# Pre-norm weight rows made by transposes and kept in PSUM, transposes of x ahead of the plain products, and other planned times for the first loads

## The chip, the cores and the metric

The kernel runs on one core of a Trainium2 chip. The metric is the device time of one execution in microseconds (us); of several runs the median counts. A core has five engines that run side by side, each with its own queue, in order: TensorE (PE, with its weight loads as PEld), VectorE (DVE), ScalarE (ACT), GpSimd (POOL) and SyncE (SP), which here issues most of the DMAs. They meet only through semaphores. Matrix products and transposes are PE's; in this kernel they write to banks of 128 x 512 float32 in PSUM, which ACT and DVE empty. The other tiles are in SBUF.

## The reference

One layer with four token mixers side by side, merged by gates. Only its head matters for the change: the residual stream (16 meta tokens, then 1024 tokens of width 1024) is normalised with the weight `pre_norm_g`, and one wide product makes the inputs of all branches.

```python
h_res = jnp.concatenate([meta, x], axis=1)          # L = 16 + 1024 rows of D_MODEL = 1024
...
def rms_norm(x, g):
    xf = x.astype(jnp.float32)
    y = xf * lax.rsqrt(jnp.mean(xf * xf, axis=-1, keepdims=True) + EPS)
    return (y * g.astype(jnp.float32)).astype(x.dtype)
...
h = rms_norm(h_res, pre_norm_g[i])
z = h @ w_in[i]
(pv, pg, cq, ckv, kr, mg, cu, cg, sbcx, sg, gl) = split_cols(z)
...
m = (gts[:, :, 0] * y_a + gts[:, :, 1] * y_b + gts[:, :, 2] * y_c + gts[:, :, 3] * y_d)
h_res = h_res + rms_norm(m @ w_o[i], post_norm_g[i])
```

## The kernel before

**A planner sets the order.** The code does not issue instructions as it runs. `record` (L287) notes each with its engine, tiles and dependences, and `flush` (L326) plays all noted instructions through a table of costs (`cost`, L266) and issues them in the order that results; `issue` (L321, called in L324) is why nearly every row of the profile has line 324. Each engine takes the ready instruction with the lowest number, where `ahead` lifts some. A load counts as landed at a planned time (L406): the pipe's time, the bytes and 4500 ns; `slow` adds `extra` nanoseconds to the moment at which its users may be planned. The table only orders instructions. On the chip the engines wait for semaphores, whatever the table thought.

**Dummies.** Where PE has nothing ready, the planner appends a transpose of the identity into an unused bank, `ps_w` (L381 to 386, `keep_busy`), and counts it as 108 ns. This goes on until the last product of the first pair of blocks has run (L1183). Once appended, a dummy stands in PE's queue and is executed, whether PE has something better to do by then or not.

**The start** (L698 to 770). SP loads eight tiles of x (128 tokens each, 512 KB), the weight row `gB`, `pre_norm_g` broadcast to 128 partitions (512 KB written), and the first columns of `w_in` (`raw_kv`, two blocks of 320 KB). For tiles t and t + 4 together, `parts(t)` makes squares with sums on ACT (`junk`), the reciprocal root on DVE and POOL (`rsx`), the scaling by `rsx` and `gB` on DVE, in halves of 512 columns (`scaled`, L714), and then the transposes: `operand_of` (L721) makes four 128 x 128 transposes on PE into a bank (two `ps_x` and one `ps_y` in turn), copies the result on ACT to the high part of an operand and subtracts on DVE for the low part. Every float32 operand here is such a pair, and a product is three matmuls for each 128 rows. `sums_of(t)` forms four differences of the x tiles on POOL, in place, and transposes them into the operands T1, T2 and T4; the wide product is done in the manner of Strassen with seven products for eight (`unit`, L568), whose weight blocks `prep` (L540) makes by sums on DVE (`ss`) and splits on ACT and POOL. `meta` does the same for the 16 meta tokens, `xm`.

**The plain products** (`plain`, L613) compute the columns `ckv` and `kr` directly, 96 matmuls for U0 (the first 256 tokens of each half) and 96 for U1. The order of the calls before: `parts(0)`, `parts(1)`, plain U0, `parts(2)`, `parts(3)`, `meta`, plain U1, then `sums_of` for all t, then the last transposes into T3, then the units. In a unit, the bank `ps_pc` is used twice: the eviction `z` on DVE must have read the first result before the second product may be added to it, and it needs `u3`, an eviction of `ps_pb`.

Everything after (the remaining blocks, attention over 8 heads, the output products) is not touched in the code.

Of the kernel before, what the change touches and what calls it, by code (L numbers as in the profile page):

```python
# [21 lines left out]
F32 = mybir.dt.float32  # L22
# [3 lines left out]
ALU = mybir.AluOpType  # L26
# [4 lines left out]
P = 128  # L31
D = 1024
# [161 lines left out]
class Plan:  # L194
# [131 lines left out]
    def flush(self):  # L326
# [38 lines left out]
        while events:  # L365
# [11 lines left out]
            for e in self.free:  # L377
# [3 lines left out]
                if o is None:  # L381
                    if e == "PE" and self.idle and self.ops[self.idle[1]]["end"] is None:
                        order.append(self.idle[0])
                        self.free[e] = t + 108
                        heapq.heappush(events, (self.free[e], 1, 0))
                    continue
                ready[e].remove((o["prio"], o["i"]))
# [13 lines left out]
                if o["op"] == "dma_start":  # L401
                    if self.pipe is None:
                        self.pipe = max((x["done"] for x in self.ops if x["op"] == "dma_start"
                                         and "done" in x and x["start"] <= t), default=0)
                    o["done"] = self.pipe = max(self.pipe, t) + o["bytes"]
                    land = self.pipe + o["bytes"] + 4500  # L406
                    o["end"] = land + o["extra"]
                    if o["eng"] != "POOL":
                        self.landed.append(land)
                    heapq.heappush(events, (land, 1, 0))  # L410
# [19 lines left out]
def trunk_kernel(ctx, tc, a):  # L430
# [76 lines left out]
    def bank(tag="x"):  # L507

        return psum.tile([P, 512], F32, tag=tag, bufs=2 if tag == "x" else 1, name=f"ps_{tag}")
# [103 lines left out]
    def plain(w, c0, n, out):  # L613

        for j, bs in enumerate(((B11, B21), (B12, B22))):
            for i, m in enumerate((P, 64)):
                ps = bank(("pa", "pb", "pc", "pd")[2 * j + i])[:m, :n]
                for h, b in enumerate(bs):
                    product(ps, w[h][i], b, c0, n, h == 0, h == 1)
                with plan.ahead(EVAC):  # L620
                    out(i, j, ps, None, None)
# [62 lines left out]
    def wload(i, c, n=2 * P):  # L684

        t = raw("raw")
        SP.dma_start(t[:, :, :n], w_in[:, KH * i:KH * (i + 1), c:c + n])
        return t
# [3 lines left out]
    def load_x(t):  # L692
# [2 lines left out]
                 raw("x").rearrange("p k c -> p (k c)") if t == 0 else  # L695
                 wp.tile([P, D], F32, tag="blk", bufs=7, name="x"))
        SP.dma_start(xt[t], a["x"][0, P * t:P * (t + 1), :])
    load_x(0)  # L698
    load_x(4)
    gB = tp.tile([P, D], F32, tag="conv", bufs=1, name="gB")  # L700
    SP.dma_start(gB, a["pre_norm_g"][0].partition_broadcast(P))
    load_x(1)
    load_x(5)
    raw_kv = [wload(i, C_CKV, P + 32) for i in range(2)]
    for t in (2, 6, 3, 7):
        load_x(t)
    ssx = const.tile([P, 16], F32, name="ssx")
    rsx = const.tile([P, 16], F32, name="rsx")

# [3 lines left out]

    def scaled(x_, t):  # L714
        n = x_.shape[0]
        for s in (slice(0, 512), slice(512, D)):
            DVE.scalar_tensor_tensor(x_[:, s], x_[:, s], rsx[:n, t:t + 1], gB[:n, s], op0=ALU.mult, op1=ALU.mult)

    turn = [0]

# [30 lines left out]
            operand_of(b, t, src)  # L751

    def meta():
        xm = wp.tile([NM, D], F32, tag="blk", bufs=7, name="xm")
        SP.dma_start(xm, a["meta_tokens"])
        square(xm, 8)
        rsqrt_mean(rsx[:NM, 8:9], ssx[:NM, 8:9], D)
        scaled(xm, 8)
# [39 lines left out]
        w_kv[i].append(kr[:, i])  # L798
    parts(1)
    out_kv = [out_raw(("ckv", "kr"), *u) for u in (U0, U1)]  # L800
    plain(w_kv, *U0, out_kv[0])
    parts(2)
    parts(3)
    meta()
    plain(w_kv, *U1, out_kv[1])
    for t in range(4):
        sums_of(t)
    for t in range(4):
        operand_of(T3, t, xt[t + 4][:, :512])
    prow = w1([P, P], name="prow")  # L810
    for r0, n, src in rows:
# [358 lines left out]
        (C_MG, ("mg0", "mg1"), out_silu),  # L1170
        (C_MG + 2 * P, ("mg2", "mg3"), out_silu),
    ] + [(C_GL + P * g, g, None) for g in range(0, 32, 2)]
    w = prep(pairs[0][0])
    for i, (_, names, kind) in enumerate(pairs):
        with plan.ahead(3000):
            nxt = prep(pairs[i + 1][0]) if i + 1 < len(pairs) else None
# [394 lines left out]
```

## Time and profile before

| | |
|---|---|
| median of 3 runs | 1052.6 us (1050.21 to 1053.01) |
| the profiled execution | 1056.61 us |
| its span, first to last instruction | 1054.6 us |
| mean granted clock of PE | 0.990 |
| first transpose of x on PE | 16.42 us |
| first product of the first unit | 62.27 us |
| last dummy | 72.6 us |

A row of a time line gives the start, the length, the engine, the line, the operation with its tiles as out<-in, the shapes, how many follow each other, and in brackets how long the engine was idle before it and what it waited for. Lengths of matmuls are those of the pipeline; the distance from one start to the next is what one costs PE. A row of groups ends with the busy time in us, the mean of one in ns, and the idle time ahead of it; a row of one tile's operations has the count, then the shortest, median and longest in ns, then the first and last start. A row of a window has the window, its length, then the busy time of PE, PEld, DVE, ACT and POOL with counts, the granted clock (1.00 is full), the DMA share and GB/s.

### The profile page before, as it was taken

The numbers are of one execution on the slowest core, as the hardware profiler recorded it, in microseconds if no ns is written. First come the engines' busy times: TensorE is split into PE (matmuls) and PEld (weight loads), VectorE is DVE, ScalarE is ACT, GpSimd is POOL, SyncE is SP. The second block draws the span as 40 slices with busy tenths as digits, with TensorE's granted clock in tenths as the row PEclk, the third lists the DMA queues.
The fourth block names the chain that finished last, engine by engine and source line by source line (L and its number), as shares of the span: only waits on it lengthen the run. The fifth ranks groups of instructions, "written<-read, shape, count | busy, mean of one in ns | idle before, by whom it ended". The sixth has DMA issues, their size and how long they took to land.

```text
span 1054.6 us, 15499 instructions
## 1 busy us (share of the span) xinstructions
PE 1024.6 (97%) x5310; PEld 858.8 (81%) x5310; DVE 725.0 (69%) x1078; ACT 428.1 (41%) x861; POOL 640.1 (61%) x582
## 2 busy tenths in 40 slices
PE   9999999999999999999999999989998989999997
PEld 9999899889888787887777778868887877678885
DVE  4865499699998998899644554266776787586232
ACT  5452333334433444533544444216655544233111
POOL 4847766657767777798867966226687866412000
PEclk9999999999999999999999999999999989999999
DMA  7033545856576655756487564987568654596221
GB/s 249 20 88 114 156 159 189 255 189 217 156 253 215 223 172 168 240 189 197 149 252 217 194 195 135 321 279 241 152 172 251 181 151 141 143 357 232 97 80 60
DMA packets 124703, 196.33 MB, mean 186 GB/s; under 512 B 19466, under 2 KB 78969, under 8 KB 123280
## 3 DMA queue, kind: packets, MB, share of 16 engines
q1 hardware_dynamic: 120016, 178.56, 53.9%
q10 hardware_dynamic: 4320, 15.73, 3.9%
q8 instruction: 42, 0.69, 0.3%
q0 software_dynamic: 288, 1.05, 0.2%
q14 instruction: 37, 0.30, 0.1%
HBM read 125.78 MB, written 69.53 MB: 185 GB/s over the span
## 4 chain that ended last, share of the span: by engine, by line
PE 44%; DVE 7%; DMA 4%; issue 3%; POOL 2%; ACT 0%; SPq 0%; POOLq 0%; ACTq 0%; DVEq 0%
PE ps_o L324 12%; PE ps_y L324 9%; PE ps_s L324 7%; PE ps_pb L324 4%; PE ps_pc L324 4%; PE ps_pa L324 4%; DVE conv L324 3%; PE ps_pd L324 2%; DMA whl<-w_out_mla 1%; PE ps_x L324 1%; DMA kt<-kr 1%; DMA th<-th 1%; DVE ss L324 1%; POOL S L324 1%; POOL A L324 0%
## 5 line engine op out<-in xcount | busy, mean ns | idle before, releaser
L324 PE MATMUL ps_pb<-T,S 128*128 128x512 f32 (+2 forms) x792 | 178.4, 367 | 1.7 <-DVE u L324 1.4
L324 PE MATMUL ps_pa<-B,A 128*128 128x512 f32 (+2 forms) x792 | 174.3, 364 | 0.0
L324 POOL TENSOR_TENSOR S<-ss,S 128x512 fp32r<-128x512 f32 x84 | 122.8, 1476 | 81.9 <-ACT S L324 77.5
L324 PEld LDWEIGHTS ps_pb<-T,S 128*128 128x128 f32 x792 | 135.6, 190 | 28.1 <-DVE u L324 2.0
L324 POOL TENSOR_TENSOR A<-raw,A 128x512 fp32r<-128x512 f32 x84 | 123.8, 1482 | 54.7 <-ACT A L324 51.9
L324 PEld LDWEIGHTS ps_pa<-B,A 128*128 128x128 f32 x792 | 135.4, 189 | 24.5 <-issue 0.5
L324 DVE SCALAR_TENSOR_TENSOR conv<-conv,par 128x512 f32<-128x512 f32 x120 | 149.2, 1243 | 2.1
L324 POOL TENSOR_TENSOR pt<-p,pt 128x512 fp32r<-128x512 f32 (+4 forms) x112 | 103.0, 948 | 25.9 <-ACT pt L324 16.2
L324 PE MATMUL ps_y<-bo,whl 128*128 128x512 f32 x288 | 86.6, 408 | 2.5 <-DVE m L324 2.5
L324 PE MATMUL ps_pc<-T,S 128*128 128x512 f32 (+2 forms) x396 | 88.9, 365 | 0.0
L324 PE MATMUL ps_pc<-B,S 128*128 128x512 f32 (+2 forms) x396 | 86.3, 362 | 2.4 <-DVE z L324 2.4
L324 ACT ACTIVATE p<-ps_s 128x512 f32<-128x512 f32 (+4 forms) x112 | 50.0, 447 | 89.6 <-DVE ps_s L324 36.8
L324 PE MATMUL ps_pd<-T,A 128*128 128x512 f32 (+2 forms) x396 | 85.6, 362 | 0.0
L324 PE MATMUL ps_s<-qt,kt 100*128 100x512 f32 (+4 forms) x336 | 74.9, 341 | 6.6 <-DVE qt L324 3.8
L324 PEld LDWEIGHTS ps_pc<-B,S 128*128 128x128 f32 x396 | 67.7, 189 | 15.0 <-DVE z L324 2.6
L324 PEld LDWEIGHTS ps_pd<-T,A 128*128 128x128 f32 x396 | 67.6, 188 | 12.2
L324 PEld LDWEIGHTS ps_pc<-T,S 128*128 128x128 f32 x396 | 67.7, 190 | 11.6
L324 PE MATMUL ps_o<-pt,vt 128*128 128x512 f32 (+4 forms) x336 | 76.1, 333 | 0.9 <-POOL pt L324 0.9
L324 ACT ACTIVATE S<-ss 128x512 fp32r<-128x512 f32 x84 | 50.7, 628 | 62.0 <-DVE ss L324 32.6
L324 PEld LDWEIGHTS ps_s<-qt,kt 100*128 100x128 f32 x336 | 58.0, 188 | 19.9 <-DVE qt L324 5.0
L324 PEld LDWEIGHTS ps_o<-pt,vt 128*128 128x128 f32 x336 | 53.1, 175 | 13.2 <-POOL pt L324 1.8
L324 ACT ACTIVATE z<-z,par 128x512 f32<-128x512 f32 x48 | 34.7, 722 | 67.8 <-DVE z L324 66.9
(332 smaller groups left out, 1861.7 us busy)
## 6 DMA issues: line engine op xcount, KB each, us to landing
raw<-in_w_in_dram SPq DMA_DIRECT2D x56, 512.0 KB
th<-z ACTq DMA_DIRECT2D x30, 512.0 KB
th<-th SPq DMA_DIRECT2D x24, 512.0 KB
whl<-w_out_mla SPq DMA_DIRECT2D x32, 256.0 KB
v<-vhl SPq DMA_DIRECT2D x16, 384.0 KB
qt<-q SPq DMA_DIRECT2D x16, 384.0 KB
bo<-bo SPq DMA_DIRECT2D x6, 1024.0 KB
vt<-v SPq DMA_DIRECT2D x8, 768.0 KB
```

The lines of the kernel that those rows point to most:

```text
L324: getattr(self.handle[o["eng"]], o["op"])(*map(real, o["args"]), **{k: real(v) for k, v in o["kw"].items()})
```

## The change

1. The weight `pre_norm_g` is no longer loaded as 128 equal rows. A tile `g8` of 8 x 128 (4 KB) is loaded on ACT's queue, transposed on PE, copied to `gC` (128 x 8), and each of its columns, broadcast, is transposed again: eight transposes give the 128 equal rows in two PSUM banks, `ps_pc` and `ps_pd`, where they stay until all of x and `xm` is scaled. `scaled` reads its weight from there.
2. `plain` uses the banks `pa` and `pb` for both halves of its columns, since `pc` and `pd` are taken.
3. The planner counts a dummy as 160 ns. A negative `extra` moves a load's planned landing itself, and the first loads are given -2000 ns. The load of the meta tokens moves up among them.
4. The calls are reordered: `parts(2)`, `parts(3)` and `meta` stand ahead of plain U0; the transposes of `sums_of` for t = 0, 1 and part of T3, then of `sums_of` for t = 2, 3, stand ahead of plain U1; the first `prep` is called between them.

```diff
-                        self.free[e] = t + 108
+                        self.free[e] = t + 160
...
-                    land = self.pipe + o["bytes"] + 4500
-                    o["end"] = land + o["extra"]
+                    land = self.pipe + o["bytes"] + 4500 + min(0, o["extra"])
+                    o["end"] = land + max(0, o["extra"])
...
-                ps = bank(("pa", "pb", "pc", "pd")[2 * j + i])[:m, :n]
+                ps = bank(("pa", "pb")[i])[:m, :n]
...
-    load_x(0)
-    load_x(4)
-    gB = tp.tile([P, D], F32, tag="conv", bufs=1, name="gB")
-    SP.dma_start(gB, a["pre_norm_g"][0].partition_broadcast(P))
-    load_x(1)
-    load_x(5)
-    raw_kv = [wload(i, C_CKV, P + 32) for i in range(2)]
-    for t in (2, 6, 3, 7):
-        load_x(t)
+    g8 = const.tile([KD, P], F32, name="g8")
+
+    with plan.slow(-2000):
+        load_x(0)
+        ACT.dma_start(g8, a["pre_norm_g"][0].rearrange("(k p) -> k p", p=P))
+        load_x(4)
+        load_x(1)
+        load_x(5)
+        raw_kv = [wload(i, C_CKV, P + 32) for i in range(2)]
+        for t in (2, 6, 3, 7):
+            load_x(t)
+        xm = wp.tile([NM, D], F32, tag="blk", bufs=7, name="xm")
+        SP.dma_start(xm, a["meta_tokens"])
+
+    gC = const.tile([P, KD], F32, name="gC")
+    pt = bank("y")
+    PE.transpose(pt[:, :KD], g8, ident[:KD, :KD])
+    DVE.tensor_copy(gC, pt[:, :KD])
+    gB = [bank(tag) for tag in ("pc", "pd")]
+    for k in range(KD):
+        PE.transpose(gB[k // KH][:, P * (k % KH):P * (k % KH + 1)], gC[:, k:k + 1].to_broadcast([P, P]), ident)
...
-        for s in (slice(0, 512), slice(512, D)):
-            DVE.scalar_tensor_tensor(x_[:, s], x_[:, s], rsx[:n, t:t + 1], gB[:n, s], op0=ALU.mult, op1=ALU.mult)
+        for i in range(2):
+            s = slice(512 * i, 512 * (i + 1))
+            DVE.scalar_tensor_tensor(x_[:, s], x_[:, s], rsx[:n, t:t + 1], gB[i][:n], op0=ALU.mult, op1=ALU.mult)
...
-    plain(w_kv, *U0, out_kv[0])
     parts(2)
     parts(3)
     meta()
+    plain(w_kv, *U0, out_kv[0])
+    for t in range(2):
+        sums_of(t)
+    w = prep(C_CU)
+    for t in range(2):
+        operand_of(T3, t, xt[t + 4][:, :512])
+    for t in range(2, 4):
+        sums_of(t)
     plain(w_kv, *U1, out_kv[1])
-    for t in range(4):
-        sums_of(t)
-    for t in range(4):
+    for t in range(2, 4):
         operand_of(T3, t, xt[t + 4][:, :512])
...
-    w = prep(pairs[0][0])
```

What the planner makes of it shows in the order of each engine's queue. First PE, from its first instruction on; `ps_w` are the dummies, `ps_x` and `ps_y` the transposes of x, `ps_pa<-B,kv` a plain product. Before:

```order
L324 MATMUL ps_w<-ident 128x128 x114
L324 MATMUL ps_x<-ident,x 128x128 x4
L324 MATMUL ps_y<-ident,x 128x128 x4
L324 MATMUL ps_x<-ident,x 128x128 x4
L324 MATMUL ps_w<-ident 128x128 x15
L324 MATMUL ps_x<-ident,x 128x128 x4
L324 MATMUL ps_w<-ident 128x128 x26
L324 MATMUL ps_y<-ident,x 128x128 x4
```

and now:

```order
L324 MATMUL ps_w<-ident 128x128 x17
L324 MATMUL ps_y<-ident,g_137 128x8
L324 MATMUL ps_w<-ident 128x128 x5
L324 MATMUL ps_pc<-ident,gC 128x128 x4
L324 MATMUL ps_pd<-ident,gC 128x128 x4
L324 MATMUL ps_w<-ident 128x128 x36
L324 MATMUL ps_x<-ident,x 128x128 x4
L324 MATMUL ps_y<-ident,x 128x128 x4
L324 MATMUL ps_x<-ident,x 128x128 x4
L324 MATMUL ps_w<-ident 128x128 x9
L324 MATMUL ps_x<-ident,x 128x128 x4
L324 MATMUL ps_w<-ident 128x128 x10
```

Of the 114 dummies ahead of the first transpose of x, 58 are left, and nine transposes for the weight rows came in. In the whole queue there were 244 dummies; there are 98.

Second POOL, around the power that finishes the scale of the meta tokens (`rsx` of 16x1); the numbers tell the tiles of x apart. Before, where x_139 and x_147 are tiles 0 and 4:

```order
L324 TENSOR_TENSOR x_139<-x_139,x_147 128x512
L324 TENSOR_TENSOR rsx_258<-rsx_258,mhalf_137 128x2
L324 TENSOR_TENSOR x_163<-x_169,x_163 128x512
L324 TENSOR_TENSOR rsx_258<-rsx_258,mhalf_137 128x2
L324 TENSOR_TENSOR rsx_258<-rsx_258,mhalf_137 16x1
L324 TENSOR_TENSOR x_169<-x_169 128x512
```

and now, where x_165 and x_156 are tiles 5 and 1, and x_188 and x_181 tiles 6 and 2:

```order
L324 TENSOR_TENSOR rsx_234<-rsx_234,mhalf_141 128x2
L324 TENSOR_TENSOR x_165<-x_165,x_156 128x512
L324 TENSOR_TENSOR x_156<-x_156,x_165 128x512
L324 TENSOR_TENSOR x_181<-x_188,x_181 128x512
L324 TENSOR_TENSOR x_188<-x_188 128x512
L324 TENSOR_TENSOR x_188<-x_188,x_181 128x512
L324 TENSOR_TENSOR x_181<-x_181,x_188 128x512
L324 TENSOR_TENSOR rsx_234<-rsx_234,mhalf_141 16x1
L324 TENSOR_TENSOR x_207<-x_215,x_207 128x512
```

The power for the meta tokens stood behind 5 of the 16 differences of x; now it stands behind 12.

Third DVE, in the second half of the first unit pair; `u2`, `u3` and `z` are evictions of a unit's banks, `ss` and `raw` the sums for the next weight block. Before:

```order
L324 TENSOR_TENSOR u3_1225<-ps_pb_1139,a__1143 128x272
L324 TENSOR_TENSOR ss_1158<-raw_1054,ss_1158 128x4x128
L324 TENSOR_TENSOR z_1266<-ps_pc_1176,u3_1225 128x272
L324 TENSOR_TENSOR z_1266<-ps_pd_1219,u3_1225 128x272
L324 COPY par_1279<-ps_x_1250 128x111
```

and now:

```order
L324 TENSOR_TENSOR u2_1071<-ps_pb_1019,a__1023 128x272
L324 TENSOR_TENSOR ss_975<-raw_870,ss_975 128x4x128
L324 TENSOR_TENSOR u3_1112<-ps_pb_1019,a__1023 128x272
L324 TENSOR_TENSOR z_1124<-ps_pc_1062,u3_1112 128x272
L324 TENSOR_TENSOR z_1124<-ps_pd_1102,u3_1112 128x272
```

The last sum of the block stood between `u3` and the eviction of `ps_pc`; now it stands ahead of `u3`.

More of the change, by code (lines that the diff above doesn't have):

```diff
@@ L753, in meta @@
     def meta():
-        xm = wp.tile([NM, D], F32, tag="blk", bufs=7, name="xm")
-        SP.dma_start(xm, a["meta_tokens"])
         square(xm, 8)
```

## The prediction

> **What bounds the kernel now.** I read the page's busy shares first, then TensorE's (PE's) waits, then the time line of its first 100 us.
>
> ```profile
> PE 1024.6 (97%) x5310; PEld 858.8 (81%) x5310; DVE 725.0 (69%) x1078; ACT 428.1 (41%) x861; POOL 640.1 (61%) x582
> PE ps_s L324 <- DVE qt L324: 3.8, 3, 3.3
> PE ps_pc L324 <- DVE z L324: 2.4, 1, 2.4
> ```
>
> PE is busy 97% of the span, and its largest wait for one cause is 3.8 us in total. So the time is what stands in PE's queue, and the span can only fall if instructions leave that queue, or a wait goes. But 244 of the instructions are dummies:
>
> ```profile
> L324 PE MATMUL ps_w<-ident x244: 271/273/477, 1.4 to 72.6; 128*128 128x128 f32 x122
> 1.44 15.14 PE L324 MATMUL ps_w<-ident 128*128 128x128 f32 x114 [1.44 <-POOL mhalf L324]
> 16.42 0.60 PE L324 MATMUL ps_x<-ident,x 128*128 128x128 f32 x4
> 16.85 0.60 PE L324 MATMUL ps_y<-ident,x 128*128 128x128 f32 x4
> 19.80 3.00 PE L324 MATMUL ps_w<-ident 128*128 128x128 f32 x26
> 22.64 0.60 PE L324 MATMUL ps_y<-ident,x 128*128 128x128 f32 x4
> ```
>
> The columns are start, length, engine, line, operation. The dummies transpose the identity into a bank that nobody reads; the planner puts one in wherever it believes that PE has nothing to do. They fill the queue whether the belief holds or not. 114 stand ahead of the first transpose of x, at 16.42, though its data are there far sooner:
>
> ```profile
> 4.66 1.06 ACT L324 ACTIVATE junk<-x 128x1024 bf16<-128x1024 f32 x1 [2.57 <-DMA x<-in_x_dram]
> 5.96 1.06 ACT L324 ACTIVATE junk<-x 128x1024 bf16<-128x1024 f32 x1
> 7.47 0.71 POOL L324 TENSOR_TENSOR rsx<-rsx,mhalf 128x2 f32<-128x2 f32 x1 [5.60 <-DVE rsx L324]
> 8.90 2.74 DVE L324 SCALAR_TENSOR_TENSOR x<-x,rsx,gB 128x512 f32<-128x512 f32 x4 [1.59 <-DMA gB<-in_pre_norm_g_dram]
> ```
>
> The first half of x tile 0 is scaled one operation (2.74/4 = 0.69) after 8.90, at 9.6. PE spends 6.8 us more on dummies because the planner expected x later. Warm dummies cost (22.64 - 19.80)/26 = 0.109 us each by their spacing (0.27 is one's length in the pipeline), and transposes of x the same: 16.85 - 16.42 = 0.43 for four.
>
> **The change, step by step.** Each sum is against the profiled execution, 1056.61 us (its span, 1054.6, and 2.0 around it); it is 4.0 above the median of the timed runs, 1052.6.
>
> *Ahead of the first transpose of x.* The new order has 58 dummies and 9 transposes for the weight rows there, 67 instead of 114. 47 fewer at 0.109 are 5.1 us: it would start at 16.42 - 5.1 = **11.3**. Are its data there? The weight column now is 4 KB on ACT's own queue; the row for the first x tile, 512 KB, bounds it from above: landed by 4.66. PE comes to its transpose after 17 dummies:
>
> ```profile
> 0.00:5.00 5.00, 3.56 (x17) 3.56 (x18) 0.06 (x1) 1.62 (x2) 1.20 (x10) 1.00 0.56 206
> 5.00:10.00 5.00, 5.00 (x41) 5.00 (x40) 1.27 (x3) 1.97 (x4) 0.71 (x1) 1.00 0.93 312
> ```
>
> That is at 5.0 (17 in 3.56 us, a slow rate of 0.21; by 10 us it is the warm one). The weight rows stand in PSUM some 14 transposes later, near 7.5, before the scale at 7.47 + 0.71 = 8.2. So the first half of x is ready near 9.0, and dummies still set 11.3. Were the column as late as the old 512 KB row, 8.9, the nine transposes and one scaling would end near 11; nothing changes. Ends for this term: 2.0 (if the data were 3.1 late, as long as ACT waits for the next x tile in the 10.24 row below) and 6.8; I take 5.1.
>
> [...]
>
> *Later dummies.* 130 follow the first transpose in the old order, 40 in the new: 90 x 0.109 = **9.8 us** leave the queue. The planner now gives a dummy 160 ns where it takes 109, so where the planner is right about the data, PE stands idle for up to 40 x 0.051 = 2.0. The transposes of x that moved between the plain products are what takes the dummies' place; the number of products and of x transposes stays.
>
> *The stall at 91.6.*
>
> ```profile
> 88.46 5.12 DVE L324 TENSOR_TENSOR ss<-raw,ss 128x512 f32<-128x512 f32 x1
> 90.54 2.49 POOL L324 TENSOR_TENSOR A<-raw,A 128x512 fp32r<-128x512 f32 x2
> 93.99 2.03 PE L324 MATMUL ps_pc<-B,S 128*128 128x272 f32 x12 [2.36 <-DVE z L324]
> 95.81 1.05 PE L324 MATMUL ps_pb<-T,S 128*128 128x256 f32 x4
> 96.00:97.00 1.00, 1.00 (x7) 1.00 (x6) 0.55 (x3) 0.95 (x3) 0.24 (x1) 0.50 0.61 107
> 99.60 1.59 PE L324 MATMUL ps_pb<-T,S 128*128 128x256 f32 x12
> L324 DVE TENSOR_TENSOR ss<-raw,ss x28: 675/1686/5123, 70.4 to 654.6; 128x512 f32<-128x512 f32 x28
> ```
>
> A DVE sum of two SBUF tensors takes 5.12 while POOL runs without a break, where the same line takes 0.675 at best and 1.69 in the median; the eviction behind it comes late, PE is idle for 2.36, and then the granted clock falls to 0.50. The 33 products from 93.99 to 99.60 take 5.61; at 0.119 each (the spacing further down) they would take 3.9, so 1.7 more are lost. In the new order this sum stands one eviction earlier: 42 products follow before PE needs the bank, where 32 did (1.2 us more), but one more eviction of 0.4 stands between. At the median length there is no stall, and I take it as gone: **4.0 us**. At 5.12 a stall of 1.6 would be left, with its slow clock. Ends: -1 (POOL's run there is one product of the rotary tables longer) and 4.0.
>
> *The scaling.* Its second operand is now in PSUM.
>
> ```profile
> L324 DVE SCALAR_TENSOR_TENSOR x<-x,rsx,gB 128x512 f32<-128x512 f32 x16 | 17.4, 1133 | 1.6 <-DMA gB<-in_pre_norm_g_dram 1.6
> L324 DVE SCALAR_TENSOR_TENSOR ckv<-ckv,par,ps_x 128x512 f32<-128x512 f32 x2 | 1.5, 748 | 2.6 <-PE ps_x L324 2.6
> L324 DVE SCALAR_TENSOR_TENSOR conv<-conv,par x120: 736/1182/3602, 134.0 to 497.7; 128x512 f32<-128x512 f32 x120
> L324 POOL TENSOR_TENSOR x<-x 128x512 f32<-128x512 f32 x16 | 23.6, 1476 | 2.4 <-PE ps_x L324 1.6
> 29.93 1.30 POOL L324 TENSOR_TENSOR x<-x 128x512 f32<-128x512 f32 x1
> ```
>
> The same form with a PSUM operand takes 748; sixteen cost 12.0 instead of 17.4, and POOL's differences of x beside them should come near 1.30 instead of 1.476. This is off PE's path; it shortens the waits below. [...] The rows say 12 ns: 748 against 736 for the fastest on SBUF.
>
> *The first loads.* The 512 KB row is out of SP's queue.
>
> ```profile
> 10.24 1.06 ACT L324 ACTIVATE junk<-x 128x1024 bf16<-128x1024 f32 x1 [3.13 <-DMA x<-in_x_dram]
> 11.56 1.06 ACT L324 ACTIVATE junk<-x 128x1024 bf16<-128x1024 f32 x1 [0.17 <-DMA x<-in_x_dram]
> 12.42 0.41 POOL L324 COPY raw<-raw 128x64 f32<-128x64 f32 x2 [4.25 <-DMA raw<-in_w_in_dram]
> ```
>
> Loads land 1.3 apart (10.24, 11.56), and the row took at most 8.90 - 5.96 = 2.9. So all behind it land 1.3 to 2.9 sooner; I take the middle, 2.1: w_in's first block at 10.3.
>
> *New waits.* By PE's queue alone, the transposes of the meta tokens come after 16 groups of x at 0.435, 96 products, one more group and 39 dummies.
>
> ```profile
> 28.23 1.90 PE L324 MATMUL ps_pa<-B,kv 128*128 128x256 f32 x14
> 38.33 1.04 PE L324 MATMUL ps_x<-ident,x 128*128 128x128 f32 x8
> 12.62 0.62 ACT L324 ACTIVATE kv<-raw 128x512 fp32r<-128x512 f32 x1
> 13.31 1.27 POOL L324 TENSOR_TENSOR kv<-raw,kv 128x512 fp32r<-128x512 f32 x1 [0.48 <-ACT kv L324]
> 20.98 1.92 POOL L324 TENSOR_TENSOR kr<-raw,kr 128x256 fp32r<-128x256 f32 x2 [0.47 <-ACT kr L324]
> L324 POOL TENSOR_TENSOR rsx<-rsx,mhalf 16x1 f32<-16x1 f32 x1 | 0.6, 551 | 0.0
> L324 DVE TENSOR_TENSOR B<-ps_x,B 128x512 fp32r<-128x512 f32 x8 | 5.4, 688 | 6.8 <-ACT B L324 6.8
> 30.16 0.39 ACT L324 ACTIVATE z<-ps_pa 128x256 f32<-128x256 f32 x1
> ```
>
> 85 products in 10.10 us are 0.119 each. 11.3 + 7.0 + 11.4 + 0.4 + 4.3 = 34.4. They need the meta tokens' scale, and POOL is in order: before it stand four small copies (0.8), two of kv (2.5), two of kr (1.9), three powers (2.1) and 12 differences of x (15.6), then its own power, 0.55. With 0.6 for ACT's first kv that is 10.3 + 24.1 = 34.4, and two scalings later, 35.9: a wait of **1.5**. DVE holds a second: in the same 23 us it has 12 scalings at 0.75 and 16 evictions at 0.69, 20 us, and PE's three transpose banks turn only as fast; I put **1.7** there. Ends of all new waits: 0, and 8 (POOL at 1.476: 2.1 more; the loads only 1.3 sooner: 0.8; one more stall with its slow clock: 2.4 + 1.7). I take 3.2.
>
> The plain products now use two banks for four results. The next result enters a bank after 23 products and four groups (4.5 us), then 24 and three (4.2); ACT's copy takes 0.4, so I cost it at nothing. That cover goes if ACT runs over 4 us late.
>
> **Sum:** 5.1 + 9.8 + 4.0 - 3.2 = 15.7 us. 1056.6 - 15.7 = 1040.9 for an execution like the profiled one; against the median, 1052.6 - 15.7 = **1036.9**. What follows is the same work on a PE with hardly an idle place, so it should move up whole. The planner's order changes there too, and with it the waits, of which the two quoted first are the largest: I allow 5 either way.
>
> **Rivals.** (1) *DVE kept waiting by POOL.*
>
> ```profile
> L324 DVE TENSOR_TENSOR ss<-raw x28: 679/684/1876, 62.1 to 648.4; 128x512 f32<-128x512 f32 x28
> ```
>
> The sums of two SBUF tensors for the first weight block move under POOL's long run of differences, where they used to stand in its pause (the first at 62.1, at full speed); or the stall at the second block comes back. Price: one stall, 4.0, is 1041; two give 1036.9 + 8 = 1045. Against it: half of these first sums take 0.684 or less, and none over 1.88. (2) *The start hardly moves*: the 67 transposes stay at the 0.21 of the first 5 us and end at 15.5, so that 0.9 of the 5.1 is left, or the first x is held by its data: 1041. Against it, the spacing of 0.109 in the trace. [...] (3) *Later stages lose*: the new order costs 5 to 10 more in the attention stage: 1042 to 1047. (4) *Slower, by the banks of the plain products.* At four reuses PE waits for ACT, which is in order with squares of x and the copies. It decides from ACT 4.2 to 4.5 us late on; to lose 15.7 + 3.2, each reuse must cost 4.7: 3.0 idle and 1.7 of slow clock. That would be ACT over 7 us late four times: 1056. ACT is busy 41%, so little speaks for it.
>
> **How the numbers follow.** Forecast 0.58 (1031 to 1041), (1) 0.22, (2) 0.08, (3) 0.07, (4) 0.03, none of these but within 0.3% for causes spread over all stages 0.02. 0.3%, 3.2 us, is about what a measurement can tell from no change: faster 0.94, same 0.03, slower 0.03. The range takes in the forecast with 3 more below for waits that go in the later stages, and (1) and (2) above: 1028 to 1046.
>
> **What would show it.** Right: the first transpose of x starts near 11 and not 16.4; 98 dummies; the scaling's mean is near 750; no PE wait over 2 us before 100, and no clock under 0.9 there; the first unit's products start near 57 (62.27 before, the row below). Wrong: PE waits on DVE or POOL of over 5 us in total before 80; a granted clock of 0.5 after one; or the first 100 us as forecast, and the gain lost past 690.
>
> ```profile
> 62.27 1.66 PE L324 MATMUL ps_pa<-B,A 128*128 128x256 f32 x12
> ```

## The result and the profile after

| | before | after |
|---|---|---|
| median (range), us | 1052.4 (1050.2 to 1053.0) | 1026.5 (1025.4 to 1028.0) |
| profiled execution, its span, us | 1056.6, 1054.6 | 1026.5, 1024.7 |
| mean granted clock of TensorE | 0.990 | 0.998 |

The ratio of the times is 0.9758, 95% interval 0.9739 to 0.9777. The change took 25.9 us by the medians; the profiled executions lie 30.1 apart, because that of before was 4.0 above its median. Executions of one kernel differ, and with them the clock that PE was granted: of 25 later executions of the kernel before, with a median of 1054.5, one had a span of 1049.8 us at a mean clock of 0.996 and another 1058.6 at 0.987. The forecast was 15.7 us less than before, 1036.9; the time lies below its range (1028 to 1046).

The busy shares, the filling transposes (fillers for short, "dummies" in the prediction) and the opening of TensorE's (PE's) time line, all of the kernel after; columns as above, with the idle time ahead of a row and its releaser in brackets:

```profile
PE 1002.0 (98%) x5173; PEld 836.5 (82%) x5173; DVE 711.1 (69%) x1079; ACT 427.0 (42%) x861; POOL 638.9 (62%) x582
```

```profile
L324 PE MATMUL ps_w<-ident x98: 271/273/477, 1.4 to 37.5; 128*128 128x128 f32 x98
```

```profile
7.61 4.09 PE L324 MATMUL ps_w<-ident 128*128 128x128 f32 x36
11.54 0.60 PE L324 MATMUL ps_x<-ident,x 128*128 128x128 f32 x4
...
35.23 0.42 PE L324 MATMUL ps_x<-ident,xm 16*128 16x16 f32 x4
...
36.59 0.29 PE L324 MATMUL ps_x<-ident,xm 16*128 16x16 f32 x2 [0.31 <-ACT hm L324]
37.20 0.23 PE L324 MATMUL ps_x<-ident,xm 16*128 16x16 f32 x1 [0.31 <-ACT B L324]
...
39.39 0.63 PE L324 MATMUL ps_x<-ident,x 128*128 128x128 f32 x4 [0.26 <-DVE T L324]
...
56.17 1.66 PE L324 MATMUL ps_pa<-B,A 128*128 128x256 f32 x12
...
76.08 1.68 PE L324 MATMUL ps_pc<-B,S 128*128 128x272 f32 x12
...
97.40 2.94 PE L324 MATMUL ps_pa<-B,A 128*128 128x512 f32 x12
```

The first transpose of x starts at 11.54 (forecast 11.3), the first unit's products at 56.17 (forecast near 57). The product that stood idle for 2.36 us before (`ps_pc<-B,S` of 272 columns, at 93.99) follows its neighbours at 76.08 with no idle time in brackets. Apart from the 1.44 us ahead of its very first instruction, PE waits nowhere in the opening longer than 0.31.

To see where the 30 us came from, I take places that both kernels pass: the first product of 512 columns into `ps_pa` (by then the opening with all filling transposes is over), the last product into `ps_pd` (end of the first stage), the first attention product, the first output product, and the last product of all. In the kernel before, the rows of three of them are:

```profile
115.44 2.97 PE L324 MATMUL ps_pa<-B,A 128*128 128x512 f32 x12
...
681.08 0.71 PE L324 MATMUL ps_s<-kt,qt 96*128 96x144 f32 x4
...
908.43 2.33 PE L324 MATMUL ps_y<-boM,whl 128*128 128x512 f32 x9
```

and in the kernel after the last two are:

```profile
661.63 0.58 PE L324 MATMUL ps_s<-kt,qt 96*128 96x144 f32 x3
...
878.96 2.33 PE L324 MATMUL ps_y<-boM,whl 128*128 128x512 f32 x9
```

| place | before | after | sooner by |
|---|---|---|---|
| first product of 512 columns | 115.4 | 97.4 | 18.0 |
| last `ps_pd` product | 678.0 | 658.6 | 19.4 |
| first attention product | 681.1 | 661.6 | 19.5 |
| first output product (`ps_y<-boM`) | 908.4 | 879.0 | 29.4 |
| last product of all | 1046.3 | 1016.5 | 29.8 |

So in the two profiled executions the opening gave 18.0 and **the attention stage gave 10.0**, from 227.3 us to 217.3, though no line of its code was changed. The output stage moved up whole. This is PE's idle time inside the attention stage of the kernel before, with the granted clock of the stretches behind it (windows: PE, PEld, DVE, ACT, POOL busy, clock, DMA share, GB/s):

```profile
804.03 4.07 PE L324 MATMUL ps_s<-qt,kt 100*128 100x512 f32 x11 [3.29 <-DVE qt L324]
846.44 0.70 PE L324 MATMUL ps_s<-qt,kt 100*128 100x400 f32 x1 [1.95 <-DVE mx L324]
```

```profile
800.00:820.00 20.00, 16.71 (x83) 13.72 (x82) 11.91 (x27) 10.71 (x22) 15.10 (x15) 0.91 0.76 238
840.00:860.00 20.00, 17.91 (x87) 15.12 (x86) 15.68 (x30) 6.87 (x18) 13.01 (x17) 0.83 0.64 184
```

3.29 and 1.95 idle, and the clock below 1.00 costs 20 x 0.09 + 20 x 0.17 = 5.2 us more. Over the whole stage PE is idle for 12.2 us before and 6.4 after. The same part of the stage after: the longest wait for `qt` or `mx` is 0.44, and the clock stays full.

```profile
834.75 2.70 PE L324 MATMUL ps_s<-qt,kt 100*128 100x512 f32 x10 [0.44 <-DVE qt L324]
```

```profile
780.00:800.00 20.00, 18.86 (x100) 15.14 (x99) 14.03 (x38) 12.44 (x26) 17.63 (x19) 1.00 0.77 248
820.00:840.00 20.00, 19.56 (x104) 16.14 (x103) 18.14 (x41) 10.75 (x26) 13.15 (x16) 1.00 0.76 222
```

Two things differ in that stage although its code is the same. The planner, which orders it by its own estimates, starts from another state at the end of the first stage and writes another order. And the tiles of the stage lie in memory that the first stage leaves, so a tile can be loaded only when the block beneath it is done with. The start of the stage fits this. SyncE's queue issues the loads of the gate tiles `th`, before:

```profile
675.67 0.32 SPq L324 DMA_DIRECT2D th<-th  x1
...
681.27 0.82 SPq L324 DMA_DIRECT2D th<-th  x2
```

and after:

```profile
651.06 0.43 SPq L324 DMA_DIRECT2D th<-th  x1
...
653.48 0.32 SPq L324 DMA_DIRECT2D th<-th  x1
```

Against the first attention product, the second load leaves 0.2 us behind it before, and 8.2 us ahead of it after. What DVE waits for these loads in the kernel before, and PE for the product `m` that DVE makes of them (us in total, times, longest):

```profile
DVE m L324 <- DMA th<-th: 5.1, 2, 3.3
PE ps_y L324 <- DVE m L324: 2.5, 1, 2.5
```

After, PE waits 0.2 us for `m`:

```profile
PE ps_y L324 <- DVE m L324: 0.2, 1, 0.2
```

### The profile page after: what moved, and what is told of

Its sections match the earlier page's. It is cut to its first block, busy times and chain, and to the rows that moved or that the text cites. A ratio compares the mean times of both kernels' runs of the same rounds, so it can differ in the third digit from the quotient of the medians.

```text
span 1024.7 us, 15229 instructions
## 1 busy us (share of the span) xinstructions
PE 1002.0 (98%) x5173; PEld 836.5 (82%) x5173; DVE 711.1 (69%) x1079; ACT 427.0 (42%) x861; POOL 638.9 (62%) x582
## 4 chain that ended last, share of the span: by engine, by line
PE 53%; DVE 3%; DMA 3%; issue 2%; POOL 1%; SPq 0%; ACT 0%; POOLq 0%; DVEq 0%; ACTq 0%
PE ps_o L324 13%; PE ps_y L324 9%; PE ps_s L324 7%; PE ps_pb L324 7%; PE ps_pc L324 7%; PE ps_pa L324 6%; PE ps_pd L324 3%; PE ps_x L324 1%; DMA whl<-w_out_mla 1%; DMA kt<-kr 1%; DMA th<-th 1%; DVE conv L324 1%; DVE m L324 1%; DVE th L324 0%; SPq L324 0%
## 5 line engine op out<-in xcount | busy, mean ns | idle before, releaser
L324 PE MATMUL ps_pb<-T,S 128*128 128x512 f32 (+2 forms) x792 | 174.4, 363 | 0.5 <-DVE u L324 0.5
L324 PE MATMUL ps_pa<-B,A 128*128 128x512 f32 (+2 forms) x792 | 171.9, 362 | 0.0
L324 POOL TENSOR_TENSOR S<-ss,S 128x512 fp32r<-128x512 f32 x84 | 120.5, 1447 | 77.0 <-ACT S L324 71.1
L324 DVE SCALAR_TENSOR_TENSOR conv<-conv,par 128x512 f32<-128x512 f32 x120 | 143.0, 1192 | 1.9
L324 POOL TENSOR_TENSOR pt<-p,pt 128x512 fp32r<-128x512 f32 (+4 forms) x112 | 105.6, 971 | 28.8 <-PE ps_s L324 12.4
L324 PEld LDWEIGHTS ps_pd<-T,A 128*128 128x128 f32 x396 | 67.2, 188 | 12.2 <-issue 0.2
L324 PEld LDWEIGHTS ps_pc<-T,S 128*128 128x128 f32 x396 | 66.7, 188 | 11.1
L324 PE MATMUL ps_s<-qt,kt 100*128 100x512 f32 (+4 forms) x336 | 71.0, 331 | 1.9 <-DVE qt L324 1.4
L324 PEld LDWEIGHTS ps_s<-qt,kt 100*128 100x128 f32 x336 | 55.9, 183 | 14.3 <-DVE qt L324 2.6
L324 ACT ACTIVATE A<-raw 128x512 fp32r<-128x512 f32 x84 | 52.4, 626 | 34.6 <-PE ps_pd L324 20.2
```

What stands on the lines that cost most here:

```text
L324: getattr(self.handle[o["eng"]], o["op"])(*map(real, o["args"]), **{k: real(v) for k, v in o["kw"].items()})
```

## Experiments on the attention stage

Three theories for the ten microseconds: the **order** that the planner writes; the **memory** under `th`; or the **sooner start** itself. A fourth, noise, is that the profiled execution of before was only a bad one. In the kernels named aattn or battn the order of the attention and output stages is a fixed list, taken from the kernel after or before, with the places of its buffers:

```diff
+            seq, slots = ORDERS[self.nf]
...
+            for j in seq:
+                self.issue(self.ops[i0 + j])
```

**The kernel after with the attention order of the kernel before** (x1_after_battn):

> The changed kernel with the instruction order of the attention stage (and the slots of its buffers) taken over from the kernel before; nothing else differs. Theory 'order': the stage from the first product of attention to the last ahead of the output products took 227.3 us before (681.1 to 908.4) and 217.4 after (661.6 to 879.0) because the planner, starting from shifted times, made another order; then this kernel has the old stage, 222 to 228 us, waits of over 2 us in it and a granted clock under 0.9 somewhere, and takes 1032 to 1037. Theory 'start': the shorter stage comes with the earlier start whatever its order; then 1025 to 1028. Theory 'noise': the profiled execution before was only a bad one; then 1025 to 1029 too, and the next run, the kernel before with the new order, stays at 1051 to 1053.

Measured: 1033.5 (1032.0 to 1034.5), 7.0 above the kernel after; the stage takes 226.0 us. (The two were timed on different occasions; the kernel before took 1054.5 beside this one and 1052.4 beside the kernel after, so the 7.0 may be some 2 us less.) The waits are back as they were, in the waits of PE (total, times, longest):

```profile
PE ps_s L338 <- DVE qt L338: 3.9, 4, 3.3
PE ps_s L338 <- DVE mx L338: 2.5, 2, 2.0
```

The sooner start is in this kernel in full, so it does not make the stage short; with the old order the stage is long again.

**The kernel before with the attention order of the kernel after** (x2_before_aattn):

> The kernel before with the attention stage's order taken over from the changed kernel. Theory 'order': the stage takes 217 to 219 us, without a clock under 0.95, and the kernel 1043 to 1047. Theory 'start' or 'noise': 1051 to 1053.

Measured: 1051.3 beside 1054.5 for the kernel before on this chip, ratio 0.9964 (0.9939 to 0.9989). The stage takes 224.7, a gain of 2.6, where I had expected 8 or more; the time is what the theories "start" and "noise" forecast. The order alone is not enough. PE's largest wait, and SyncE's first load of `th` in the stage:

```profile
PE ps_y L338 <- DVE m L338: 2.9, 1, 2.9
```

```profile
678.72 0.32 SPq L338 DMA_DIRECT2D th<-th  x1
```

It leaves 0.2 us behind the first attention product (678.53). The list is that of the kernel after, but the memory beneath is that of the kernel before. This led to the experiments on memory, below.

**The kernel before, with one number of the planner shifted** ahead of the attention stage, to see how much the order is worth by chance. x3_before_pool tells it that GpSimd is free 1.5 us later:

```diff
+    plan.free["POOL"] += 1500
```

> The kernel before; only the planner's time at which POOL is free when it starts on the attention stage is raised by 1500 ns, so that it finds another order for that stage. If an order is a matter of luck of some us ('order'), the time moves by 1 to 8 us, either way, with the waits in that stage; if orders are all about the same, 1051 to 1053.

x4_before_level sets all engines to the latest of them:

```diff
+    plan.free = {e: max(plan.free.values()) for e in plan.free}
```

> The kernel before; only the planner's times at which the engines are free at the start of the attention stage are set to the latest of them. As the run with POOL's time alone: under 'order' the time moves by 1 to 8 us, either way, with the waits in that stage; otherwise 1051 to 1053.

Measured: 222.4 us in the stage and 1050.7 for the first, ratio 0.996 (0.9937 to 0.9982); 225.9 and 1054.3 for the second, 0.9995 (0.9975 to 1.0016). In the first, a number that describes nothing real takes 5 us off the stage and 4 off the time; the second leaves the time as it was, against what the theory of luck in the order forecast.

**The memory alone, and both.** The buffers of `th` go to a pool behind all others, where no late block of the first stage lies:

```diff
+    hp = pool(two, name="hp", reuse_waits="tile")
...
-                th = fp.tile([P, NT], F32, tag="th", bufs=3, name="th")
+                th = hp.tile([P, NT], F32, tag="th", bufs=3, name="th")
```

First with the order of before, fixed (m1_before_th):

> The kernel before with its own attention order, instruction by instruction, but the three buffers of th (the gate tiles loaded back from memory in the attention stage) placed in memory that no late block of the first stage uses. In the kernel before two of the three lie where the last weight blocks of the first stage lie, their loads leave only 5.4 us ahead of the first attention product and after it, DVE waits 5.1 us for them and the product 2.5 us for DVE (m). Theory 'memory': that wait goes (2.5 us of idle time), and the slower clock behind idle places may go with it: attention stage (first ps_s product to first ps_y<-boM product) 227.3 less 2 to 5, so 222 to 225, and 1048 to 1050. Rival 'order only': the loads are early but another wait of the stage's start takes its place, 226 to 228, no change of the time.

Then with the order of the kernel after, fixed (m2_before_aattn_th):

> The kernel before with the attention order of the kernel after, and the buffers of th placed in memory that is free early. With that order alone the stage took 224.7 us (217.4 in the kernel after), with a wait of 2.9 us for m at its start and th loads leaving only from 0.2 us after the first attention product on (in the kernel after from 10.5 us ahead of it). Theory 'order and memory together': the stage takes 217 to 220 us, no wait over 0.5 us for m, and the time is 5 to 7 us below the same kernel without the move, 1044 to 1047. Rival 'order alone': 224 to 225 and 1051.

Measured: 1052.2 for the first, ratio to before 0.9975 (0.9957 to 0.9993), stage 225.3; 1048.7 for the second, 0.9945 (0.9925 to 0.9965), stage 218.8. In the first, the wait for `m` only falls from 2.5 to 2.4, against my expectation, and the loads still leave late, the second at 677.49 where the stage starts at 679.25. In this order they stand in SyncE's queue behind two weight loads that leave only at 676.65:

```profile
676.65 0.80 SPq L338 DMA_DIRECT2D whl<-w_out_pool  x2
677.49 0.91 SPq L338 DMA_DIRECT2D th<-th  x2
```

In the second the time lies above the 1044 to 1047 expected and a wait for `m` is left, but the stage is as short as expected. The loads leave early, as in the kernel after:

```profile
669.01 0.43 SPq L338 DMA_DIRECT2D th<-th  x1
671.51 0.43 SPq L338 DMA_DIRECT2D th<-th  x1
```

```profile
PE ps_y L338 <- DVE m L338: 1.2, 1, 1.2
```

The four cells of attention stage on the opening of before, in us:

| | order of before | order of after |
|---|---|---|
| `th` in its old memory | 227.3 | 224.7 |
| `th` in memory that is free early | 225.3 | 218.8 |

By these profiles the two are worth 2.6 and 2.0 alone, and together 8.5 of the 10.0. The timed executions show no such surplus: by their ratios 3.8 (1.2 to 6.4) for the order alone, 2.6 (0.7 to 4.5) for the memory alone, and 5.8 (3.7 to 7.9) for both. Each cell is one profile, and the slow clock makes part of its size. As an estimate I count half of the time that PE is busy at a clock of 0.50 as lost: in the kernel before, products of 512 columns (`ps_y<-bo,whl`) start 0.43 us apart at that clock (851.20 to 852.05), and 0.24 apart at the full one (25 from 690.00 to 695.96). In this stage that is 5.0 us in the kernel before, 3.4 in x2, 2.7 in m1 and nothing in m2. Without the loss the four cells, row by row, are 222.3, 221.3, 222.7 and 218.8, so that order and memory together are worth 3.5 there. And the loss is in part luck. The same ten products stand behind the same three waits (0.4, 0.4 and 0.33 us) in x2 and in m2; in x2 the clock falls to half behind them, in m2 it does not. x2, each row with the window that follows:

```profile
804.58 3.87 PE L338 MATMUL ps_s<-qt,kt 100*128 100x512 f32 x10 [0.33 <-DVE qt L338]
806.00:808.00 2.00, 2.00 (x6) 1.53 (x6) 1.68 (x5) 1.97 (x5) 0.96 (x1) 0.50 1.07 300
```

and m2:

```profile
801.36 2.71 PE L338 MATMUL ps_s<-qt,kt 100*128 100x512 f32 x10 [0.33 <-DVE qt L338]
802.00:804.00 2.00, 2.00 (x10) 1.50 (x9) 1.97 (x6) 1.54 (x3) 0.18 (x1) 1.00 1.07 362
```

Not all of it is luck: the order of before loses 5.0, 6.5 and 2.7 us in its three profiles (before, x1, m1), that of after 0 to 3.4 in its seven. The kernel after has the other order and the early loads, though no line of the change names either.

**The kernel after with `th` moved**, so that the planner orders the stage once more (m3_after_th):

> The kernel after with the buffers of th in memory that is free early; the planner sees that and puts the attention stage in another order than in both kernels. Theory 'the order is drawn anew with every small change': the stage falls somewhere between 217 and 226 us (the six seen so far: 217.4 to 227.3), without a wait for m over 0.5 us: 1026 to 1034. Rival 'the kernel after has a good order for a reason (early start)': 217 to 219 again, 1025 to 1028.

Measured: 1028.7 (1027.6 to 1030.5), stage 219.6; both are 2.2 above the kernel after. That is within the first expectation and just above the rival's ranges. The memory gives the kernel after nothing more, and with another order it is no faster (its longest wait for `mx` is 1.5, where the kernel after has 0.4, and the clock is at half for 3.4 us).

## Experiments on the opening

These four keep the attention order of the kernel after. What they show is read at the first product of 512 columns; six kernels with the opening of before have it between 114.1 and 115.5, three with that of after between 96.6 and 97.4, so a difference of one microsecond means little.

**Only the planner's numbers** (s1_table), the kernel before with

```diff
-                        self.free[e] = t + 108
+                        self.free[e] = t + 160
...
+    with plan.slow(-2000):
```

> The kernel before with nothing but the changed numbers of the planner (a filling transpose counted as 160 instead of 108, first loads taken to land 2000 ns sooner); weight row still by its 512 KB load, old order of calls; attention stage kept in the order of the kernel after. It holds 160 filling transposes instead of 244, 65 instead of 114 ahead of the first transpose of x. Theory 'the filler sets the start': each of them costs 0.109 us of the queue, so the first transpose of x comes at 16.42 - 49 x 0.109 = 11.1, the last product into ps_pd of the first stage at 678.0 - 84 x 0.109 = 668.8, and the idle place at the first pair of tiles (2.4 us at the second half of the first stage's opening, DVE late) stays. Rival 'the data set the start': the 512 KB weight row is late on the queue of transfers, a wait takes the filler's place, first scaled product or transpose of x waits 2 us or more, and the last product comes at 672 or later.

**The kernel after with the old order of calls** (s2_oldcalls):

```diff
+    plain(w_kv, *U0, out_kv[0])
     parts(2)
     parts(3)
     meta()
-    plain(w_kv, *U0, out_kv[0])
...
+    for t in range(4):
+        sums_of(t)
```

> The kernel after with the old order of calls (plain products of the first tile pair ahead of the transposes of tiles 2 and 3, all four sums after both plain parts, first weight preparation at its old place); attention order of the kernel after. It holds 120 filling transposes instead of 98, 58 ahead of the first transpose of x as in the kernel after. Theory: the new order of calls is worth its fillers, 22 x 0.109 = 2.4 us, and the idle place at the first pair with the slow clock behind it (4.0): first transpose of x at 11.5, last product into ps_pd at 658.6 + 2.4 + 4.0 = 665.0. Rival: the idle place went with the sooner start alone, 661.0. Rival: the fillers only stood where the engine would have waited, 658.6 to 660.

**The kernel after with 108 again** (s3_dummy108):

```diff
-                        self.free[e] = t + 160
+                        self.free[e] = t + 108
```

> The kernel after with a filling transpose counted as 108 again; attention order of the kernel after. 144 filling transposes instead of 98, 86 instead of 58 ahead of the first transpose of x. Theory 'the filler sets the start': first transpose of x at 11.54 + 28 x 0.109 = 14.6, last product into ps_pd at 658.6 + 46 x 0.109 = 663.6. Rival 'they fill what would be idle': first transpose near 11.5 to 12, last product within 1 us of 658.6.

**The kernel after with the weight rows loaded into SBUF** (s4_gbdma):

```diff
+        SP.dma_start(gBt, a["pre_norm_g"][0].partition_broadcast(P))
...
-    gB = [bank(tag) for tag in ("pc", "pd")]
+    gB = [gBt[:, 512 * i:512 * (i + 1)] for i in range(2)]
```

> The kernel after with the weight rows in SBUF by one 512 KB load (as in the kernel before) and without the nine transposes that make them; attention order of the kernel after. 162 filling transposes instead of 98 and 9 weight transposes gone, 65 ahead of the first transpose of x. Theory: what the transposed weight rows buy is the fillers, (64 - 9) x 0.109 = 6.0 us: first transpose of x near 11.3, last product into ps_pd at 664.6, no idle place at the first pair. Theory 2 'the port': the scaling with both operands in SBUF is held by GpSimd, DVE falls behind again, an idle place of 2 us with slow clock after it returns near 75, last product at 668 or later. Rival: the fillers stood in for waits, 660.

| kernel | fillers | first transpose of x | first product of 512 columns | last `ps_pd` product | attention stage | time |
|---|---|---|---|---|---|---|
| before | 244 | 16.4 | 115.4 | 678.0 | 227.3 | 1052.4 |
| s1_table | 160 | 11.3 | 109.1 | 674.5 | 222.8 | 1050.2 |
| s4_gbdma | 162 | 11.1 | 105.6 | 667.8 | 222.5 | 1044.2 |
| s3_dummy108 | 144 | 14.3 | 101.5 | 664.3 | 220.4 | 1035.6 |
| s2_oldcalls | 120 | 10.7 | 98.4 | 660.0 | 225.0 | 1034.2 |
| after | 98 | 11.5 | 97.4 | 658.6 | 217.3 | 1026.5 |

The times of s1 to s4 are medians of 8, 2, 2 and 4 executions. The kernel before took 1054.6 beside them, and s1's ratio to it, 0.9977 (0.9943 to 1.0011), can't be told from no change.

- s3 agrees with "the filler sets the start": 28 more ahead of x delay it by 2.8, 46 more cost 4.1 at the product of 512 columns and 5.7 at the stage's end (5.0 expected).
- s1 does not. The first transpose of x comes at 11.3 as expected, but 84 fillers less are worth 6.3 and not 9.2. The idle place of the first pair stays (2.25 us, at 87.80), and 3.5 is left at the stage's end. Of the 2.8 lost in between, 1.6 is a wait of PE for `S` that the kernel before does not have. The rival, 672 or later, is the nearer.
- s2 misses the other way: with the old order of calls the kernel loses 1.3 at the stage's end where 6.4 was expected (1.0 of it up to the product of 512 columns). Most of the miss is the stall: the idle place comes back with 0.60 us and no slow clock, and not with 4.0. The 22 additional fillers do cost something: from the first transpose of x to the product of 512 columns s2 takes 1.8 more than the kernel after, of 2.4 expected.
- s4: without the weight rows in PSUM 9.2 is lost at the stage's end, 8.2 of it up to the product of 512 columns; 6.0 expected. That is near the 668 of theory 2, but no idle place returns at the pair. 64 fillers more and nine transposes fewer are the expected 6.0 of the 8.2; and PE is idle for 4.2 us up to that product where the kernel after has 2.4, mostly in waits for x and `xm`, the scaled tiles. The groups of DVE show the slower scaling. With the row in SBUF (s4), and after:

```profile
L338 DVE SCALAR_TENSOR_TENSOR x<-x,rsx,gB 128x512 f32<-128x512 f32 x16 | 18.6, 1199 | 1.7 <-POOL rsx L338 1.7
```

```profile
L324 DVE SCALAR_TENSOR_TENSOR x<-x,rsx,ps_pc 128x512 f32<-128x512 f32 x8 | 5.9, 739 | 0.9 <-POOL rsx L324 0.9
L324 DVE SCALAR_TENSOR_TENSOR x<-x,rsx,ps_pd 128x512 f32<-128x512 f32 x8 | 5.9, 739 | 0.0
```

In s4 the scaling of the meta tokens starts at 41.9, in the kernel after at 33.6. So the largest part of the opening hangs on the weight row in PSUM: 8.2 (s4 to after), or 10.8 (s1 to s2, which differ also in the banks of the plain products and in the place of the meta tokens' load). The planner's numbers give 6.3 alone, and the order of calls 1.0 on top of the rest or 3.5 without the weight rows (s1 to s4, with the same two differences). That fewer fillers come with the row in PSUM is the planner's doing: its table (`cost`, and `turns` in `record`) counts a scaling with a PSUM operand as shorter and does not let it take turns with GpSimd. What the 512 KB load costs by being back in SyncE's queue was not separated from the slower scaling.

The four also show the attention stage again, each with the order of the kernel after. Where SyncE's first load of `th` leaves 10.6 or 10.9 us ahead of the first attention product (s3, s4) the stage takes 220.4 and 222.5; where it leaves 0.2 behind it (s1, s2), 222.8 and 225.0. s2 starts the stage only 1.3 us later than the kernel after, and yet PE waits 2.6 us for `m`: SyncE had stood for 10.7 us until a product into `ps_pc`, of the first stage, was done. The rows of s2, where the stage starts at 662.97:

```profile
663.16 0.32 SPq L338 DMA_DIRECT2D th<-th  x1
SPq L338 <- PE ps_pc L338: 11.9, 2, 10.7
PE ps_y L338 <- DVE m L338: 2.6, 1, 2.6
```

So an early start and the order of the kernel after do not make the short stage without early loads. Of the 9.5 us between the profiles of s2 and of the kernel after, 7.7 lie in this stage, 3.4 of them as slow clock.

**Fewer fillers still** (m4_after_th_d240), as m3 and

```diff
-                        self.free[e] = t + 160
+                        self.free[e] = t + 240
```

> As the one ahead, and a filling transpose counted as 240 instead of 160: 39 instead of 58 of them ahead of the first transpose of x. Theory 'the filler sets the start': the first transpose of x comes at 11.54 - 19 x 0.109 = 9.5, and the first product of 512 columns (97.4 in the kernel after) 2 to 3 us sooner. Rival 'the data set it by now': the first scaled block is ready at about 9.5 (scaling halves of 0.74 us from 8.1 on) and later transposes wait for DVE, so that the opening gains under 1 us. The attention order is again another one: 1024 to 1034.

Measured: 1047.5 (1046.0 to 1049.0). The first transpose of x comes at 9.13, after a wait of 0.56 for its data, and the next ones wait too (0.91 for `B`, 0.48); the product of 512 columns comes at 97.1, where m3 has it at 96.9. The data set the opening now. That the kernel is 18.8 slower than m3 has another cause, at the start of its attention stage:

```profile
675.43 2.90 PE L324 MATMUL ps_y<-bo,whl 128*128 128x512 f32 x6 [16.28 <-DMA whl<-w_out_pool]
```

SyncE issues nothing between 644.67 and 659.73, since a store (`w_out_mla<-whl`) at the head of its queue waits, and all first loads of the attention stage stand behind it; in the kernel after that store leaves at 642.78. Why the store is late in this order I have not followed up.

## Why the prediction was off

*Ahead of the first transpose of x:* 5.1 forecast, 4.9 measured (16.42 to 11.54). Right; s3 shows the price of a filler there (28 for 2.8 us), and m4 that there was only some 2 us more to have before the data come.

*Later fillers, 9.8, and the stall, 4.0:* with the first term 18.9, and the opening gained 18.0. Right, as a sum and by its parts: 146 fillers fewer and nine transposes more are 14.9, PE's idle time went down by 2.1, and a slow clock that cost 1.7 is gone, 18.7 in all. The stall went as forecast; its sum `ss<-raw,ss`, 5.12 before, takes 1.76:

```profile
72.61 1.76 DVE L324 TENSOR_TENSOR ss<-raw,ss 128x512 f32<-128x512 f32 x1 [1.06 <-POOL S L324]
```

But a filler taken away is worth its 0.109 us only when its place has work. s1 shows it: 84 fewer without the weight rows in PSUM gave 6.3, and not 9.2. I had entered the faster scaling as off PE's path and shortening waits; by s1 and s4 the weight row in PSUM is also what lets the removal of fillers pay, whether by the scaling or by the load that it saves.

*New waits, −3.2:* mis-sized; 0.9 measured (0.31, 0.31 and 0.26 above). PE came to the meta tokens at 35.23 against the forecast 34.4, and their data were there: GpSimd's power for them started at 33.06, not 33.9, and the second scaling started at 34.30. GpSimd's two `kr` took 1.43 and not 1.9, and its differences of x took 1.29 each, the good end of the estimate.

*"A PE with hardly an idle place, so it should move up whole", 5 either way:* this step failed. The attention stage of before was not such work: of its 227.3 us PE is idle for 12.2, with places of 3.29, 2.47 and 1.95 us, and a slow clock behind the first and the last costs 5.0 more. After, PE is idle for 6.4 and the clock is full; the stage lost 10.0 us, twice what I had allowed, and the range had only 3 below the forecast for it. The difference in order had been seen and put down as five microseconds of either sign, with a rival only for a loss (rival 3). That loads of the next stage may leave sooner or later had not been thought of. The runs show the stage between 217.3 and 227.3, and the kernel before sat at the slow end. The idle places were to be read in the profile of before; that the new order would take them away was not. The size is that of two executions: by the timed runs the order of before costs the kernel after 7.0 (x1), or some 5 if the two occasions are allowed for, and without the attention stage the time would have come out within the range.

*The rivals:* DVE kept waiting by GpSimd (1) cost PE nothing: one of the moved sums of the first block did take 1.70 us, at 41.38, where such a sum takes 0.68 at best, but no wait of PE followed. The start did move (2): the transposes did not stay at 0.21 us. The 17 fillers from 1.44 to 5.25 take 0.22 each, the 36 from 7.61 on 0.109 again. Of the plain products' two banks (4) the waits of the opening show nothing.

By the profiled executions: forecast 15.7; 2.3 more from the waits that did not come, 1.4 in the rest of the first stage, 10.0 in attention, 0.6 at the end and around the span: 30.0 of the 30.1 measured. Of these, 5.0 in attention, 1.7 in the opening and 1.7 in the rest of the first stage are slow clock of that one execution of before.

What stays open: 1.5 of the 10.0 (218.8 against 217.3; PE waits 1.2 for `m` in the one and 0.2 in the other), how much of the slow clock is luck, and which of the many swaps in the order removes the waits for `qt` and `mx`. The kernel after with nothing changed but `th` in memory that is free late was not tried; s2 comes near it.

## What to carry to other kernels

Where a planner orders the work by its own estimates, a change at the start can draw the order of the later stages anew: before forecasting "the rest moves up", compare the later orders, list the idle places there with the slow clock behind them, and look at which memory the next stage's first loads lie in. Filler work is worth removing only up to the point where the data are there; make the data earlier first. And to attribute a gain, mark places that both kernels pass, and freeze the order of the stages that are not under test, and the places of their first tiles too. Time more than one execution of each cell before calling a sum of effects more than its parts.

## What the runs showed of the hardware

What follows an idle place of PE is no fixed price. In the kernel before, the clock stays full behind the 2.47 us that end at 690.00, and is at half for six us behind the 1.95 us that end at 846.44:

```profile
690.00:692.00 2.00, 2.00 (x9) 1.64 (x10) 0.83 (x2) 0.00 (x0) 0.00 (x0) 1.00 1.04 384
692.00:694.00 2.00, 2.00 (x10) 1.63 (x9) 1.08 (x2) 0.00 (x0) 0.00 (x0) 1.00 0.61 244
...
846.00:848.00 2.00, 1.56 (x6) 1.55 (x7) 1.28 (x4) 0.59 (x1) 0.00 (x0) 0.56 0.62 121
848.00:850.00 2.00, 2.00 (x9) 1.83 (x8) 0.30 (x1) 1.23 (x3) 1.19 (x1) 0.50 0.31 55
850.00:852.00 2.00, 2.00 (x7) 1.77 (x7) 1.64 (x4) 1.14 (x3) 2.00 (x3) 0.50 0.89 343
852.00:854.00 2.00, 2.00 (x10) 1.66 (x8) 1.29 (x3) 0.73 (x2) 1.43 (x4) 0.73 0.34 54
```

The slow windows lose 0.9 + 1.0 + 1.0 + 0.5 = 3.4 us, more than the idle place itself. After the 16.28 us of m4_after_th_d240, which end at 675.43, the clock is already at half, and stays there for 8 us, though PE is nearly without a break; this is the last slow window and the first full one:

```profile
682.00:684.00 2.00, 2.00 (x7) 1.29 (x5) 1.43 (x5) 0.00 (x0) 0.11 (x1) 0.51 1.00 385
684.00:686.00 2.00, 1.40 (x6) 0.89 (x6) 1.90 (x5) 0.00 (x0) 0.00 (x0) 1.00 1.07 342
```

In the kernel before the clock is at half for 3.4 us (95.3 to 98.7, 409.3 to 412.7, and 805.3 to 808.7) or for twice that (846.2 to 853.1), and in m4 for at least 10 us (0.50 or 0.51 in each window of two us from 674.0 to 684.0). What makes the difference between 2.47 and 1.95, or between x2 and m2 above, no run here shows.
